# Output-weight packs of a hybrid attention + PEER layer: the last pack in group A's slot, the low parts on VectorE

## The chip, the cores and the metric

One Trainium2 chip, one NeuronCore. The metric is the device time of one execution in microseconds (us), as the median of several runs. TensorE (PE in the profile, its weight loads PEld), VectorE (DVE), ScalarE (ACT), GpSimd (POOL) and the queue of SyncE (SP), which issues all the DMAs, each work through their own instructions in order and wait for each other by semaphores.

## The reference

One decoder layer for 256 tokens of width 1024, in float32. Two groups of heads mix the tokens, their outputs go through one output projection, and a PEER feed-forward layer follows.

```python
proj = rmsnorm(x, norm1_gain) @ w_in
...
o_a = nsa_mixer(...)      # group A: compressed + selected + window attention
o_b = mla_mixer(...)      # group B: multi-head latent attention
mixed = jnp.concatenate([rmsnorm(o_a, out_gain_a), rmsnorm(o_b, out_gain_b)], axis=-1) @ w_out
h = x + mixed
return h + peer_ffn(rmsnorm(h, norm2_gain), peer_w_q, peer_sub_keys, peer_u, peer_v)
```

`w_out` is 1024 x 1024. `peer_ffn` multiplies the normalised stream by `peer_w_q`, finds the best 16 of 16,384 experts per head, and works with `peer_u` and `peer_v`, 64 MB each, in dense form.

## The kernel before, in words

**Precision by splitting.** Large products are made with `float32r` operands. Each weight tile is split into a high part, `hi` (ScalarE copies the float32 tile with rounding, line 270 or 798), and a low part, `lo` = tile - `hi` (a subtraction on VectorE or GpSimd, line 272, 796 or 801). A product is then three passes on TensorE: hi x hi, hi x lo, lo x hi. A pack of output weights is 128 x 2048 floats, 1 MB; `split_pack` gives its split a slot, and `part(q, e)` splits one quarter (128 x 512) with the low part on engine `e`, GpSimd where none is named.

**Stages.** Up to about 165 us: input projection, both attention groups, output projection, second norm. Then the PEER layer: 16 tiles of `wq` (PE rows "q"), 128 tiles of `u` ("a"), 128 tiles of `v` ("y"), each loaded, split and multiplied; TensorE goes from tile to tile. The change lies in the first part.

**Slots.** SBUF is cut into slots of 128 x 4096 floats, `slot(i, ...)`, tagged b0 to b7; a new tile in a slot waits until every reader of the old one is done. Slot 2, slot 7, slot 2 again and slot 6 hold the four packs of output weights (`wo_slot`, line 997). Slot 4 holds `aS`: group A's queries and keys (`qSa`, `kHa`, `kLa`), read only by the score matmuls "sA" (lines 676 and 677). Slot 6 holds `cm`: the compressed keys, masks, and the attention outputs by token (`otok`, ring `r_ot`), which are read up to `finish` of the last group of 128 tokens (line 604 squares them, line 608 transposes them).

**Output projection.** Packs 0 and 1 (`wo0`, `wo1`) hold the rows of group B, packs 2 and 3 (`wo2`, `wo3`) those of group A; of each pair, the first holds output columns 0 to 511 and the second 512 to 1023. `split_wo(n)` is a generator that splits a pack by quarters. `wo_mm(tt, n, ab)` makes 256 output columns for one half `tt` of the tokens and one group `ab`: 12 matmuls at line 1015 against `mixT`, the transposed outputs of the group (hi at line 613, lo at line 614), and one VectorE add into `h` (line 1019). After that follow `square` (line 1024 or 1026), the transposes of `h` ("tx", line 296), their scaling (line 298), split (299, 302), and the first `wq` tile.

**Order.** From line 993 to 1127 only SP's order is written by hand; on the other engines a scheduler sets the order from the program and its dependencies. From line 1139 on the order is the one written. SP's queue loads packs 0 to 3 (line 1001), then the first five `wq` tiles (line 783; `load(0)` to `load(4)`), each waiting for its staging buffer, which an earlier split must have read.

**Attention of group A.** `unit_A(tt, rr, g)`: scores "sA", maximum "nmA" on VectorE (line 685), exponentials on ScalarE (690), transposes "pTA" (696), evacuation "PT" (598), product with the values "oA" (708), and at the end of four heads a normalisation on VectorE (714 to 721). The eight units of the second half of the tokens go first, then the four of the first half. `end_A` adds the compressed part (line 731) and calls `finish`.

Of the kernel before, what the change touches and what calls it, by code (L numbers as in the profile page):

```python
# [85 lines left out]
def body(tc, nc, ap, dbg=None):  # L86
    V, A, T, G, S = nc.vector, nc.scalar, nc.tensor, nc.gpsimd, nc.sync
# [6 lines left out]
    with ExitStack() as ctx:  # L94
# [43 lines left out]
        def small(shape, name, dt=F32, bufs=None):  # L138
            return sm.tile(shape, dt, tag=name, name=name, bufs=bufs or 2)
# [119 lines left out]
        def split_pack(r, i, w, name):  # L259

            d = slot(i, name, F32R)
            hi, lo = d[:, :8 * w], d[:, 2048:2048 + 8 * w]
            out = (hi.rearrange("p (k n) -> p k n", k=8), lo.rearrange("p (k n) -> p k n", k=8))

            def part(q, e=None, what="hl"):

                cs = slice(q * 2 * w, (q + 1) * 2 * w)
                src = r[q // 2][:, (q % 2) * 2 * w:(q % 2 + 1) * 2 * w]
                if "h" in what:
                    A.activation(out=hi[:, cs], in_=src, func=AF.Copy)  # L270
                if "l" in what:
                    (e or G).tensor_tensor(lo[:, cs], src, hi[:, cs].bitcast(F32), op=ALU.subtract)

            def half(q, e=None, what="hl"):
                cs = slice(q * 4 * w, (q + 1) * 4 * w)
                if "h" in what:
                    A.activation(out=hi[:, cs], in_=r[q], func=AF.Copy)
                if "l" not in what:
                    return
                if (e or (V, G)[q]) is V:  # L280
                    V.tensor_tensor(lo[:, cs], r[q], hi[:, cs].bitcast(F32), op=ALU.subtract)  # L281
                else:
                    part(2 * q, G, "l")
                    part(2 * q + 1, G, "l")
            half.part = part
            return out, half
# [706 lines left out]
        with tc.manual_schedule(engines={mybir.EngineType.SP}):  # L993

            side = Side(7)
            wos = {}
            wo_slot = (2, 7, 2, 6)
            s4 = [small([128, 4], "n2_s4") for tt in range(2)]

            def load_wo(n):  # L1000
# [2 lines left out]
            def split_wo(n):  # L1003
                wos[n] = split_pack(wos[n], wo_slot[n], 256, "wo%d" % n)
                for q in range(4):
                    wos[n][1].part(q, G)
                    yield

            def wo_mm(tt, n, ab):
# [66 lines left out]
            ua = [unit_A(1, (r,), g) for r in range(4) for g in range(2)]  # L1076
            side.add(*ua[:7])
            beside(split_wo(0), 1)
            load_wo(2)
            co = compress_out()  # L1080
# [4 lines left out]
            side.add(unit_C(1), *ua[7:], ea[1], unit_C(0))  # L1085
            side.add(*[unit_A(0, rr, g) for rr in ((0, 1), (2, 3)) for g in range(2)], ea[0])
            beside(split_wo(1), 1)
            load_wo(3)
            side.until(ub[-1])
            ticks[0] = 0  # L1090
            extra += [(26, lambda: (load(0), load(1), split(0), load(2), split(1)))]
            w2g, w3g = split_wo(2), split_wo(3)
            for n in range(4):
                for tt in range(2):
# [395 lines left out]
        for s in range(NQ + NU, N):  # L1490
# [14 lines left out]
            for i, tt, n, p in order:  # L1505
                jj, (hi, lo), wh = tiles[i]
                q, src = ((0, hi), (0, lo), (1, hi))[p]
# [83 lines left out]
```

## Time and profile before

| | |
|---|---|
| median of 3 runs | 964.89 us (964.03 to 970.98) |
| profiled execution, its own time | 965.19 us |
| its span, first to last instruction | 963.4 us |
| outside the span | 1.8 us |
| granted TensorE clock, mean | 0.992 |
| first `wq` matmul (PE, line 1135) | at 164.5 us |

Times in the rows are microseconds from the span's start. A row of the timeline has start, length, engine, line, operation, output<-inputs, shape and count, and in brackets the idle time of the engine ahead of it with what ended it. A row of the table by stages has for each engine the busy time and the number of instructions that start in it, then the granted TensorE clock as a share of full speed, the share of DMA time and GB/s. A float32 matmul stands as two rows in a count.

### The profile page before, as it was taken

What the parts mean: (1) busy time and instruction counts of PE and PEld (TensorE: products, weight loads), DVE (VectorE), ACT (ScalarE), POOL (GpSimd) and SP (SyncE); (2) the same over time, 40 slices, a digit from 0 to 9 for tenths busy, and PEclk for the clock granted to TensorE, in tenths of its full rate; (3) what the DMA queues carried; (4) which work ended last, traced back from release to release, by engine and by line L of the source; (5) the groups of instructions that cost most, each with busy time, mean ns of one, the idle gap of its engine ahead of it and who ended that gap; (6) DMA issues with size and microseconds to landing.
All of it is one profiled execution on the core that took longest, in us unless ns stands there. A gap on an engine that the chain in (4) does not pass through costs nothing.

```text
span 963.4 us, 17115 instructions
## 1 busy us (share of the span) xinstructions
PE 937.8 (97%) x6651; PEld 851.0 (88%) x6651; DVE 714.3 (74%) x1346; ACT 501.2 (52%) x927; POOL 171.1 (18%) x136
## 2 busy tenths in 40 slices
PE   7999998999899999999999999999999999999998
PEld 6887787999899999999999999888888888888886
DVE  6987666777979998898999995666666666666664
ACT  4667664656354365554544544544455554445552
POOL 5333224267119400000111112000000000000000
PEclk9999998999999999999999999999999999999999
DMA  8425211654566476555555556655665655665554
GB/s 328 171 88 190 74 45 48 216 159 148 152 200 202 140 222 193 163 159 171 158 171 154 166 163 185 190 195 196 196 194 188 195 192 193 197 196 194 189 191 148
DMA packets 47314, 166.73 MB, mean 173 GB/s; under 512 B 5505, under 2 KB 6529, under 8 KB 46977
## 3 DMA queue, kind: packets, MB, share of 16 engines
q1 hardware_dynamic: 47232, 165.64, 53.9%
q8 instruction: 52, 0.85, 0.4%
q14 instruction: 30, 0.24, 0.1%
HBM read 163.52 MB, written 2.10 MB: 172 GB/s over the span
## 4 chain that ended last, share of the span: by engine, by line
PE 76%; DVE 14%; issue 4%; ACT 3%; POOL 2%; DMA 2%; SPq 0%; DVEq 0%; POOLq 0%; ACTq 0%
PE y L1508 36%; PE a L1135 26%; PE q L1135 5%; PE g L1351 3%; DVE lo L801 2%; PE wo L1015 1%; DMA raw<-u 1%; PE low L314 1%; PE s L1444 1%; DVE win L281 1%; ACT hi L798 1%; DVE B L1251 1%; PE oA L708 1%; POOL b_rs L150 1%; DVE B L1252 1%
## 5 line engine op out<-in xcount | busy, mean ns | idle before, releaser
L801 DVE TENSOR_TENSOR lo<-raw,hi 128x1024 fp32r<-128x1024 f32 x236 | 289.0, 1227 | 96.0 <-ACT hi L798 93.6
L798 ACT ACTIVATE hi<-raw 128x1024 fp32r<-128x1024 f32 x266 | 280.1, 1054 | 56.3 <-DMA raw<-u 50.1
L1508 PE MATMUL y<-hi,w 128*128 128x512 f32 x1024 | 274.6, 389 | 0.0
L1135 PE MATMUL a<-xtT,hi 128*128 128x256 f32 x2048 | 260.3, 280 | 0.0
L1135 PEld LDWEIGHTS a<-xtT,hi 128*128 128x128 f32 x2048 | 243.3, 188 | 0.4 <-issue 0.4
L1508 PEld LDWEIGHTS y<-hi,w 128*128 128x128 f32 x1024 | 192.0, 188 | 40.1 <-ACT w L1238 0.2
L1508 PE MATMUL y<-lo,w 128*128 128x512 f32 x512 | 158.4, 389 | 0.0
L1135 PE MATMUL a<-xtT,lo 128*128 128x256 f32 x1024 | 138.5, 278 | 5.0 <-DVE lo L801 5.0
L1238 ACT ACTIVATE w<-B 128x256 fp32r<-128x256 f32 x128 | 53.4, 417 | 171.2 <-PE y L1508 171.0
L1135 PEld LDWEIGHTS a<-xtT,lo 128*128 128x128 f32 x1024 | 126.8, 189 | 5.6 <-DVE lo L801 5.6
L1508 PEld LDWEIGHTS y<-lo,w 128*128 128x128 f32 x512 | 96.1, 188 | 19.9
L1239 DVE TENSOR_TENSOR w<-B,w 128x256 fp32r<-128x256 f32 x128 | 54.5, 426 | 70.0 <-ACT w L1238 70.0
L801 POOL TENSOR_TENSOR lo<-raw,hi 128x1024 fp32r<-128x1024 f32 x30 | 72.3, 2416 | 52.4 <-ACT hi L798 51.8
L1483 POOL TENSOR_TENSOR B<-gl,B 128x512 f32<-128x512 f32 (+33 forms) x37 | 29.8, 805 | 253.0 <-ACT gl L1482 253.0
L1366 ACT ACTIVATE B<-g 128x64 f32<-128x64 f32 (+29 forms) x121 | 23.7, 245 | 77.0 <-DVE B L1364 77.0
L1339 DVE TENSOR_TENSOR oh<-misc,con 128x1024 f16<-128x1024 f16 x64 | 55.9, 873 | 0.0
L1476 ACT ACTIVATE B<-a 128x512 f32<-128x512 f32 (+33 forms) x59 | 28.1, 476 | 45.1 <-PE a L1135 45.1
L1343 DVE TENSOR_TENSOR oh<-oh,gf 128x1024 f16<-128x1024 f16 x64 | 44.3, 692 | 2.2
L1351 PE MATMUL g<-oh 128*128 128x128 f16 x512 | 39.7, 220 | 0.2
L1364 DVE TENSOR_TENSOR B<-g,B 128x8 f32<-128x8 f32 (+32 forms) x69 | 32.7, 479 | 6.1 <-ACT B L1476 5.9
L1135 PE MATMUL q<-xrT,hi 128*128 128x256 f32 x256 | 35.5, 283 | 0.0
L1015 PE MATMUL wo<-wo,mix 128*128 128x256 f32 x192 | 31.8, 311 | 2.6 <-ACT mix L613 1.5
(311 smaller groups left out, 897.6 us busy)
## 6 DMA issues: line engine op xcount, KB each, us to landing
raw<-u SPq DMA_DIRECT2D x128, 512.0 KB, 3.6
raw<-v SPq DMA_DIRECT2D x128, 512.0 KB, 3.6
raw<-wq SPq DMA_DIRECT2D x16, 512.0 KB, 3.5
win<-win SPq DMA_DIRECT2D x10, 512.0 KB, 8.0
w<-w SPq DMA_DIRECT2D x8, 512.0 KB, 4.0
wo<-wout SPq DMA_DIRECT2D x8, 512.0 KB, 6.5
wsm<-wu SPq DMA_DIRECT2D x1, 1280.0 KB, 9.3
xx<-x SPq DMA_DIRECT2D x4, 256.0 KB, 3.3
```

The lines of the kernel that those rows point to most:

```text
L798: A.activation(out=hi, in_=src, func=AF.Copy)
L801: e.tensor_tensor(lo, src, hi.bitcast(F32), op=ALU.subtract)
L1015: T.matmul(o, lhsT=mixT[:, ab * 4 + c, q, tsls[tt]], rhs=ww[:, (n % 2) * 4 + c, :], start=(m == 0 and c == 0), stop=(m == 2 and c == 3))
L1135: T.matmul(out, lhsT=w[:, k, :], rhs=xT[:, k, q, :], start=(n == 0 and k == 0), stop=(n == 2 and k == 7))
L1238: A.activation(out=w[:, 0, :], in_=b, func=AF.Copy)
L1239: V.tensor_tensor(w[:, 1, :], b, w[:, 0, :].bitcast(F32), op=ALU.subtract)
L1339: V.tensor_tensor(o[:, 0:2].rearrange("p a t (i two) -> p (a t) i two", two=2), iot.rearrange("p (i two) -> p i two", two=2)[:, None].broa ...
L1343: V.tensor_tensor(pairs(o[:, 2:4]), pairs(o[:, 1:2]).broadcast_to((128, 2, 4, 64, 2)), gf[:, t4, :, :, None, :].broadcast_to((128, 2, 4, 6 ...
L1351: T.matmul(b[:, i, :], lhsT=o[:, 0, i, :], rhs=o[:, 2 + q, i, :], start=(q == 0), stop=(q == 1))
L1364: V.tensor_tensor(w, bv[:, c0:m, :], w, op=ALU.mult)
L1483: (G if j < 127 else V).tensor_tensor(dst[:, :, :td], a[:, :, :td], dst[:, :, :td], op=ALU.mult)
L1508: T.matmul(ya[tt][n], lhsT=wh[:, q, tt * 128:(tt + 1) * 128], rhs=src[:, n * 512:(n + 1) * 512], start=(jj == 0 and p == 0), stop=(jj == 1 ...
```

## The change

Two edits. The fourth pack of output weights takes slot 4 (where `aS` was) in place of slot 6 (where `cm` is). And all sixteen low-part subtractions of the four packs, 128 x 512 each, go to VectorE in place of GpSimd.

```diff
             side = Side(7)
             wos = {}
-            wo_slot = (2, 7, 2, 6)
+            wo_slot = (2, 7, 2, 4)
             s4 = [small([128, 4], "n2_s4") for tt in range(2)]
...
             def split_wo(n):
                 wos[n] = split_pack(wos[n], wo_slot[n], 256, "wo%d" % n)
                 for q in range(4):
-                    wos[n][1].part(q, G)
+                    wos[n][1].part(q, V)
                     yield
```

The scheduler also places other instructions differently. In its rows `wo_1101`, `wo_1270`, `wo_1485` and `wo_1592` are the split packs 0, 1, 2 and 3. First place: ScalarE at the end of group A's attention, where pack 3 is split. Before:

```order
L795 ACTIVATE hi<-raw 128x256
L690 ACTIVATE wsm,suA<-sA,nmA 128x128
L598 ACTIVATE PT<-pTA 128x512
L690 ACTIVATE wsm,suA<-sA,nmA 128x128 x3
L795 ACTIVATE hi<-raw 128x256 x3
L598 ACTIVATE PT<-pTA 128x512
L604 ACTIVATE fe,o_ss<-cm 128x512
L1024 ACTIVATE fe,n_s_679<-xx 128x256
L270 ACTIVATE wo_1592<-wo 128x512
L613 ACTIVATE mix<-fe 128x4x128
L270 ACTIVATE wo_1592<-wo 128x512
L299 ACTIVATE xrT<-kept 128x2x128
```

Now:

```order
L270 ACTIVATE wo_1592<-wo 128x512
L690 ACTIVATE wsm,suA<-sA,nmA 128x128
L598 ACTIVATE PT<-pTA 128x512
L690 ACTIVATE wsm,suA<-sA,nmA 128x128 x3
L270 ACTIVATE wo_1592<-wo 128x512 x2
L598 ACTIVATE PT<-pTA 128x512
L270 ACTIVATE wo_1592<-wo 128x512
L795 ACTIVATE hi<-raw 128x256 x4
L1024 ACTIVATE fe,n_s_679<-xx 128x256
L604 ACTIVATE fe,o_ss<-cm 128x512
```

The four high parts of pack 3 stood behind the square of the last attention output (line 604); they now stand among the exponentials of the last unit, ahead of it.

Second place: VectorE where group B ends and the first scores of group A arrive (from line 659 on). The difference, a piece of it:

```order
 L659 TENSOR_TENSOR cm<-oB,suB 128x512
+L272 TENSOR_TENSOR wo_1101<-wo,wo_1101 128x512 x2
+L149 TENSOR_SCALAR rs_x<-o_ss 128x1
+L611 TENSOR_TENSOR fe<-oT,pp 128x512
+L685 TENSOR_REDUCE nmA<-sA 128x2
+L272 TENSOR_TENSOR wo_1101<-wo,wo_1101 128x512
+L614 TENSOR_TENSOR mix<-fe,mix 128x4x128
+L272 TENSOR_TENSOR wo_1101<-wo,wo_1101 128x512
 L560 TENSOR_SCALAR fe<-fe 128x256
-L1019 SCALAR_TENSOR_TENSOR xx<-wo,misc,xx 128x256
+L685 TENSOR_REDUCE nmA<-sA 128x2
 L561 TENSOR_TENSOR fe<-fe,cm 128x256
```

The four low parts of pack 0 come in among group B's last `mixT` split and the first maxima of group A, and the compression's steps (lines 560, 561) fall behind them.

Third place: TensorE at the end of the projection. Before:

```order
L1015 MATMUL wo<-wo_1485,mix 128x256 x17
L608 MATMUL oT<-con,cm 128x128 x4
L296 MATMUL tx<-con,xx 128x128 x2
L1015 MATMUL wo<-wo_1485,mix 128x256 x7
L1015 MATMUL wo<-wo_1592,mix 128x256 x2
L296 MATMUL tx<-con,xx 128x128 x2
L1015 MATMUL wo<-wo_1592,mix 128x256 x15
```

Now:

```order
L1015 MATMUL wo<-wo_1485,mix 128x256 x23
L1015 MATMUL wo<-wo_1592,mix 128x256 x4
L608 MATMUL oT<-con,cm 128x128 x4
L296 MATMUL tx<-con,xx 128x128 x4
L1015 MATMUL wo<-wo_1592,mix 128x256 x20
L296 MATMUL tx<-con,xx 128x128 x2
```

Matmuls with pack 3 now stand ahead of the last `oT` transposes. SP's order is unchanged.

## The prediction

> **What bounds the kernel now.** I read the page's busy times first, then a table by stages, then, for the stage of the change, the table in finer steps and the timelines.
>
> ```profile
> PE 937.8 (97%) x6651; PEld 851.0 (88%) x6651; DVE 714.3 (74%) x1346; ACT 501.2 (52%) x927; POOL 171.1 (18%) x136
> ```
>
> ```profile
> 93.80:104.50 10.70, 9.22 (x49) 6.65 (x48) 8.22 (x12) 7.26 (x23) 8.31 (x7) 0.84 0.53 181
> 104.50:118.00 13.50, 13.50 (x103) 11.10 (x102) 7.58 (x25) 9.65 (x33) 0.74 (x1) 1.00 0.17 54
> 118.00:143.10 25.10, 24.18 (x169) 20.31 (x167) 16.73 (x44) 15.87 (x55) 5.57 (x5) 1.00 0.13 43
> 143.10:149.20 6.10, 5.98 (x44) 5.07 (x43) 5.46 (x10) 3.97 (x12) 2.43 (x3) 1.00 0.02 4
> 149.20:159.20 10.00, 5.83 (x29) 5.63 (x30) 6.27 (x11) 2.20 (x7) 5.81 (x6) 0.69 0.12 49
> 164.50:236.00 71.50, 71.50 (x621) 70.65 (x620) 53.41 (x203) 43.70 (x71) 39.31 (x24) 1.00 0.54 174
> 400.00:963.00 563.00, 559.31 (x3571) 495.97 (x3569) 399.02 (x497) 278.10 (x488) 28.75 (x33) 1.00 0.57 182
> ```
>
> TensorE is busy 97% of the span. From 164.5 on, where the PEER layer starts, it has no gap for 71.5 us, and later only small ones. So whatever brings the first `wq` matmul forward moves all that follows by as much, and the end too. Ahead of that there is one bad stage: 149.2 to 159.2, with PE busy 5.83 of 10 us and a clock of 0.69. The same stage in finer steps:
>
> ```profile
> 149.20:151.40 2.20, 1.10 (x7) 0.90 (x7) 1.37 (x3) 0.77 (x2) 2.20 (x3) 1.00 0.00 0
> 151.40:154.47 3.07, 0.00 (x0) 0.00 (x0) 3.07 (x4) 0.00 (x0) 2.34 (x2) 0.77 0.00 0
> 154.47:159.20 4.73, 4.73 (x22) 4.73 (x23) 1.83 (x6) 1.43 (x5) 1.27 (x2) 0.50 0.26 103
> 159.20:161.50 2.30, 2.30 (x19) 2.30 (x18) 0.70 (x2) 0.00 (x0) 0.00 (x0) 0.85 0.04 16
> ```
>
> PE stands still for 1.10 and 3.07 us, and then runs 4.73 us at half clock. The timelines of PE, ScalarE, GpSimd and VectorE say why:
>
> ```profile
> 150.30 1.10 PE L1015 MATMUL wo<-wo,mix 128*128 128x256 f32 x7 [1.11 <-POOL wo L272]
> 154.47 0.69 PE L296 MATMUL tx<-con,xx 128*128 128x128 f32 x2 [3.07 <-DVE xx L1019]
> ```
>
> ```profile
> 145.23 0.63 ACT L604 ACTIVATE fe<-cm 128x512 f32<-128x512 f32 x1 [3.11 <-DVE cm L731]
> 146.26 0.62 ACT L270 ACTIVATE wo<-wo 128x512 fp32r<-128x512 f32 x1
> ```
>
> ```profile
> 147.29 2.96 POOL L272 TENSOR_TENSOR wo<-wo,wo 128x512 fp32r<-128x512 f32 x2
> 150.89 2.85 POOL L272 TENSOR_TENSOR wo<-wo,wo 128x512 fp32r<-128x512 f32 x2
> ```
>
> ```profile
> 131.86 0.68 DVE L614 TENSOR_TENSOR mix<-fe,mix 128x512 fp32r<-128x512 f32 x1
> 147.43 1.69 DVE L614 TENSOR_TENSOR mix<-fe,mix 128x512 fp32r<-128x512 f32 x1
> 150.28 3.74 DVE L796 TENSOR_TENSOR lo<-raw,hi 128x256 fp32r<-128x256 f32 x3 [0.83 <-POOL wo L272]
> 153.94 0.47 DVE L1019 SCALAR_TENSOR_TENSOR xx<-wo,misc,xx 128x256 f32<-128x256 f32 x1
> ```
>
> Pack 3 is not split until 146.26, when the last reader of slot 6 (line 604, the square of the last attention output) is done. GpSimd then needs 147.29 to 153.74 for its low parts, so PE waits for them at 149.2. While GpSimd streams, VectorE's own subtractions crawl: the same line 614 takes 0.68 us with GpSimd idle and 1.69 beside it, and three small line 796 take 3.74. So the add at 153.94, for which the next transposes wait, is late, and PE stands until 154.47.
>
> **The change part by part.** *Slot.* The last reader of `aS` is this matmul:
>
> ```profile
> 136.24 0.38 PE L677 MATMUL sA<-aS 64*128 64x256 f32 x1
> ```
>
> It ends at 136.6, so the high parts can start some 9.6 us earlier than 146.26. By the new order of ScalarE they go in between the exponentials of the last unit and are over by about 142. The low parts, four on VectorE at 0.68 us (the row at 131.86 has their shape and types), are 2.7 us. VectorE has room there:
>
> ```profile
> 135.00:138.00 3.00, 3.00 (x23) 2.47 (x22) 0.69 (x1) 1.92 (x9) 0.00 (x0) 1.00 0.55 178
> 138.00:142.00 4.00, 4.00 (x35) 3.79 (x33) 1.97 (x5) 3.69 (x14) 0.00 (x0) 1.00 0.00 0
> ```
>
> 2.66 of 7 us are used. Pack 3 is then complete near 143, before PE has worked through the 24 matmuls with pack 2. So the 1.10 us stall goes, and the 3.07 one with it, as nothing of GpSimd's is left beside VectorE but small steps of line 302.
>
> *Clock.* With the two stalls gone, nothing is left that lowers the clock at 154.47. Half clock for 4.73 us costs 2.37, and 0.85 over the next 2.30 us costs 0.35: 2.7 us. The clock does not drop after every gap:
>
> ```profile
> 98.00:101.00 3.00, 3.00 (x14) 2.05 (x13) 2.96 (x5) 2.16 (x9) 3.00 (x4) 0.58 0.30 123
> 60.80:62.40 1.60, 0.00 (x0) 0.00 (x0) 1.60 (x3) 0.34 (x2) 0.00 (x0) 1.00 0.84 220
> ```
>
> From 60.8 on, a TensorE that stood still for 1.60 us kept full clock, while from 98 on it ran at 0.58. The Trainium skill, "TensorE: Matmul & The Clock Gate", section "What's actually happening", says that the clock halves after an idle window of about 3.4 us, and that these windows run freely, not tied to the kernel. The row at 154.47 agrees in kind (0.50, neither more nor less), and so does the one at 60.80. By it the cold stretch is a whole number of windows, one or two, 1.7 or 3.4 us of loss here in place of my 2.7, and a rest of the stall could still catch one; that outcome is the fourth rival below.
>
> *What stays on the path.* After the change PE runs from the last "oA" at 143.1 through pack 2 and pack 3, five groups of 12 matmuls, to the end of the first group for `tt` = 0. A group with its transposes is worth the distance of these two starts, 1.65 us:
>
> ```profile
> 161.22 1.68 PE L1015 MATMUL wo<-wo,mix 128*128 128x256 f32 x12
> 162.87 1.67 PE L1015 MATMUL wo<-wo,mix 128*128 128x256 f32 x12
> 159.29 1.95 PE L1015 MATMUL wo<-wo,mix 128*128 128x256 f32 x12
> ```
>
> Five are 8.25: done at 151.35, where the row at 159.29 (the second group for `tt` = 0) has it at 159.3. That is 7.9 us, the upper end for this part. Its operand, `mixT` for `tt` = 0, is ready by about 148.2 (line 614 at 147.43 with 0.68), ahead of the 149.7 at which it is needed. The lower end is 1.1: the pack's wait alone goes, and the adds of line 1019 stay as late. I take 1.10 + 3.07 + 2.7 = 6.9, less 0.4 for a transpose that still waits for its add (one add is 0.47): 6.5.
>
> *Sixteen low parts on VectorE.* Twelve of them (packs 0 to 2) fall between 93.8 and 143.1. Twelve at 0.68 are 8.2 us more on VectorE, where the three rows of the stage table show 32.5 of 49.3 us busy; 16.8 are free. The tight spot is the beginning: 8.22 of 10.70 us up to 104.5, with GpSimd busy 8.31 beside it. There the new order puts pack 0's four (2.7 us) among the first maxima "nmA", and PE's scores wait behind those. But this is also where GpSimd stretches VectorE's steps:
>
> ```profile
> 98.03 1.14 DVE L614 TENSOR_TENSOR mix<-fe,mix 128x512 fp32r<-128x512 f32 x1
> ```
>
> Line 614 takes 0.46 more than its 0.68, and the compression's steps move behind. So the part is costed from both sides. Latest: packs 0 and 1 whole in front of the units, 8 x 0.68 = 5.4 us later. Earliest: nothing added, and the clock kept where it now falls to 0.58 (3.0 x 0.42 = 1.3; the stretch is longer than the row, so an estimate of 1.7): 1.7 earlier. Following the new order by hand, the matmuls with group B's `mixT` start a microsecond earlier and the eight units of the second half end about where they did. I take 0.
>
> *Loads.* SP's first `wq` tiles wait for buffers that these splits read (the waits of its queue, its timeline, the page's DMA row, and ScalarE's first split of such a tile):
>
> ```profile
> SPq L783 <- POOL wo L272: 20.4, 3, 12.5
> ```
>
> ```profile
> 96.00 0.33 SPq L783 DMA_DIRECT2D raw<-wq  x1
> 127.80 0.33 SPq L783 DMA_DIRECT2D raw<-wq  x1
> ```
>
> ```profile
> raw<-wq SPq DMA_DIRECT2D x16, 512.0 KB, 3.5
> ```
>
> ```profile
> 106.21 0.72 ACT L795 ACTIVATE hi<-raw 128x256 fp32r<-128x256 f32 x2
> ```
>
> The first issues when GpSimd is through with pack 0; by the new order VectorE is through with it some 2 us later, near 98, the tile lands 3.5 us after that, and its split at 106 still finds it: no cost. The fourth, at 127.80, follows pack 2 and comes earlier.
>
> *The keys.* They are loaded into the memory of the old slots, if the big tile begins where slot 0 did into slot 4, now pack 3's:
>
> ```profile
> 166.99 0.33 SPq L1227 DMA_DIRECT2D B<-keys  x1
> ```
>
> The issue comes 2.5 us after the last matmul with pack 3 (162.87 + 1.67), and by SP's unchanged order behind the spill of that product: no cost.
>
> Sum, against the profiled execution: 965.19 - 6.5 - 0 = 958.7. That execution lies 0.3 above the median of the runs, so for a median 958.4; I say 958.5.
>
> **The rivals.** *The front gains as well.* GpSimd's contention goes and the clock does not fall at 98: 1.7 more, 956.8. If the tail reaches its 7.9 too, 965.2 - 7.9 - 1.7 = 955.6. For it: the rows at 98.03 and 98.00. Against: PE still has gaps of about a microsecond near 93 and 96 in the new order.
>
> *VectorE's queue delays the units.* Packs 0 and 1 in front of the maxima cost their 5.4 less what the contention gave, about 1.5: +3.9, so 962.5. For it: VectorE is the fullest engine up to 104.5. Against: 5.9 us of VectorE are idle from 104.5 to 118.
>
> *Slower: VectorE sets the pace to 143.* All twelve low parts land on the chain score, maximum, exponential, "oA", 8.2 us later; each makes PE wait, and the clock falls again. The tail then keeps its cold stretch: -4.2 + 8.2 = +4.0, 969.2. It decides once the last "oA" is over 6.9 us late, so with more than ten of the twelve on the path. Against: the 16.8 free microseconds.
>
> *The stall comes back elsewhere.* The slot is free but pack 3 does not come early enough, or a shorter gap remains and catches a closed clock: of 6.9 only 1.10 to 4.2 go, 961 to 964. For it: ScalarE is full from 138 to 142 (3.69 of 4), and the four high parts, 2.5 us, go there. Against: PE has 24 matmuls with pack 2 to do first, which are 3.3 us.
>
> **How the numbers follow.** The forecast, 956.5 to 961, has 0.54; the front's gain 0.16; the delayed units 0.16; the returning stall 0.09; slower 0.05. Without the outermost 0.2 the range is 954.5 to 963.8. One per cent is 9.65 us, about what a measurement of this kernel can tell from no change. Faster by over that needs below 955.2, about half of the first rival: 0.09. Slower by over 1% needs more than 974.5: only the fourth case beyond its price, 0.02. Within: 0.89.
>
> **What would show it.** In the profile after, line 270 for pack 3 starts near 137; PE has no gap over 1 us from 143 to the first `wq` matmul, with clock 1.00; that matmul stands near 158 (164.5 before); line 614 takes 0.68 each time; the last "oA" ends within 2 us of 143.1. Wrong if the last "oA" ends after 146, if PE's clock still falls to 0.50 ahead of the first `wq` matmul, or if the first `wq` matmul moves and the end does not.

## The result

The changed kernel takes 955.95 us (median of 13 runs, 953.05 to 960.89), the kernel before, measured beside it, 963.27 (13 runs, 961.28 to 973.54). The ratio is 0.9912, with a 95% interval of 0.9884 to 0.9940: 0.9% faster. The interval leaves out 1, so this is a gain, though it is smaller than the one per cent that the prediction set as its mark. Medians and ranges, here and below, are of all runs, while a ratio is not their quotient: it leaves out runs over 1.5% above the fastest of their kernel. The profiled execution took 955.38 us with a span of 953.6, 9.8 less than before.

The page's busy times, after:

```profile
PE 934.6 (98%) x6651; PEld 850.0 (89%) x6651; DVE 712.9 (75%) x1362; ACT 501.0 (53%) x927; POOL 149.5 (16%) x120
```

```profile
PE 88%; DVE 8%; ACT 1%; POOL 1%; issue 1%; DMA 0%; SPq 0%; DVEq 0%; POOLq 0%; ACTq 0%
```

VectorE has sixteen instructions more (1362 for 1346) and is busy 1.4 us *less* (714.3 before). The sixteen subtractions add 10.7 us by the sum of their rows. In return lines 560, 561, 564, 614, 721 and 796, which GpSimd had stretched, take 8.2 us less together. Another 2.3 us fall away in lines 1258 and 1263 of the PEER layer, which the change does not touch, so that part of the difference is no effect of contention with these subtractions. The second line is the head of the chain that ended last: PE has 88% of it, VectorE 8%. Before it read:

```profile
PE 76%; DVE 14%; issue 4%; ACT 3%; POOL 2%; DMA 2%; SPq 0%; DVEq 0%; POOLq 0%; ACTq 0%
```

The same stretches of time as in the prediction's table, after (the work in them has moved forward; the last one now holds the first `wq` matmul):

```profile
93.80:104.50 10.70, 10.70 (x71) 7.93 (x72) 9.49 (x19) 8.94 (x29) 0.56 (x1) 1.00 0.44 151
104.50:118.00 13.50, 13.50 (x104) 11.80 (x104) 9.36 (x32) 8.55 (x32) 0.55 (x1) 1.00 0.25 80
118.00:143.10 25.10, 24.03 (x169) 20.41 (x169) 20.26 (x52) 17.53 (x59) 0.55 (x1) 1.00 0.14 43
143.10:149.20 6.10, 5.27 (x45) 5.07 (x44) 5.63 (x15) 3.74 (x13) 1.47 (x2) 1.00 0.02 7
149.20:159.20 10.00, 10.00 (x86) 9.94 (x85) 6.34 (x23) 5.47 (x20) 4.00 (x6) 1.00 0.37 117
```

Two rows stand out. From 149.2 to 159.2 PE is busy for all of the 10 us (5.83 before) at full clock (0.69 before). From 93.8 to 104.5 it is also busy all the time (9.22 before) at full clock (0.84 before). The end of the first part, on PE's timeline:

```profile
139.61 1.00 PE L708 MATMUL oA<-xx,PT 128*128 128x64 f32 x8
...
147.98 0.44 PE L296 MATMUL tx<-con,xx 128*128 128x128 f32 x2 [0.83 <-DVE xx L1019]
...
154.77 0.48 PE L1135 MATMUL q<-xrT,hi 128*128 128x256 f32 x2
```

and before:

```profile
142.28 1.00 PE L708 MATMUL oA<-xx,PT 128*128 128x64 f32 x8
164.52 0.48 PE L1135 MATMUL q<-xrT,hi 128*128 128x256 f32 x2
```

From here on two distances are used. From the start of the last "oA" to the first `wq` matmul: 22.24 us before, 15.16 after, so the tail gained 7.08. The last "oA" itself is 2.67 earlier, so the front gained too. Together 9.75. From the first `wq` matmul to the end of the span it is 798.9 before and 798.8 after: nothing was given back later.

### The profile page after: what moved, and what is told of

It is laid out like the page before. It is cut to its first block, busy times and chain, and to the rows that moved or that the text cites. A ratio compares the mean times of both kernels' runs of the same rounds, so it can differ in the third digit from the quotient of the medians.

```text
span 953.6 us, 17117 instructions
## 1 busy us (share of the span) xinstructions
PE 934.6 (98%) x6651; PEld 850.0 (89%) x6651; DVE 712.9 (75%) x1362; ACT 501.0 (53%) x927; POOL 149.5 (16%) x120
## 4 chain that ended last, share of the span: by engine, by line
PE 88%; DVE 8%; ACT 1%; POOL 1%; issue 1%; DMA 0%; SPq 0%; DVEq 0%; POOLq 0%; ACTq 0%
PE y L1508 37%; PE a L1135 35%; PE q L1135 5%; PE g L1351 3%; PE wo L1015 2%; PE oA L708 1%; PE low L314 1%; PE ak L314 1%; PE s L1444 1%; DVE win L281 1%; DVE lo L801 1%; POOL b_rs L150 1%; PE pTA L696 1%; PE sA L677 1%; DVE rq L1417 0%
## 5 line engine op out<-in xcount | busy, mean ns | idle before, releaser
L1135 PEld LDWEIGHTS q<-xrT,hi 128*128 128x128 f32 x256 | 32.1, 188 | 0.1
```

The costliest lines, as they stand in the source:

```text
L1135: T.matmul(out, lhsT=w[:, k, :], rhs=xT[:, k, q, :], start=(n == 0 and k == 0), stop=(n == 2 and k == 7))
```

## The experiments

Each kernel was measured against the kernel before on the same chip. The first four were measured together (before: 966.06, 33 runs, 961.67 to 981.16), and so were the next four (964.24, 33 runs, 962.43 to 981.48) and the last three (964.95, 11 runs, 963.04 to 978.67).

| kernel | median, us | range | ratio and interval | last "oA" | first `wq` | distance |
|---|---|---|---|---|---|---|
| before | 963.27 | 961.28–973.54 | 1 | 142.28 | 164.52 | 22.24 |
| changed | 955.95 | 953.05–960.89 | 0.9912 [0.9884, 0.9940] | 139.61 | 154.77 | 15.16 |
| e1_slot | 961.61 | 955.31–971.77 | 0.9930 [0.9884, 0.9976] | 149.69 | 165.08 | 15.39 |
| e2_vector | 956.00 | 954.30–962.38 | 0.9905 [0.9867, 0.9942] | 141.28 | 157.88 | 16.60 |
| e3_last_on_v | 962.56 | 953.88–977.07 | 0.9929 [0.9884, 0.9974] | 158.93 | 174.15 | 15.22 |
| e4_first_on_v | 955.77 | 953.66–961.43 | 0.9892 [0.9854, 0.9930] | 141.54 | 156.44 | 14.90 |
| e5_warm | 964.49 | 962.19–968.58 | 1.0004 [0.9981, 1.0027] | 143.81 | 165.17 | 21.36 |
| e6_slot_warm | 957.69 | 954.70–960.83 | 0.9913 [0.9878, 0.9948] | 140.47 | 155.86 | 15.39 |
| e7_pack0_on_v | 963.24 | 960.46–968.70 | 0.9989 [0.9963, 1.0015] | 146.62 | 165.82 | 19.20 |
| e8_tx | 955.20 | 952.35–959.45 | 0.9897 [0.9861, 0.9933] | 142.66 | 156.95 | 14.29 |
| e9_tx_warm | 956.89 | 954.13–960.01 | 0.9900 [0.9843, 0.9956] | 142.73 | 157.03 | 14.30 |
| e10_after_again | 957.39 | 954.03–960.40 | 0.9898 [0.9841, 0.9955] | 144.94 | 160.10 | 15.16 |
| e11_tx_again | 955.20 | 954.62–961.96 | 0.9894 [0.9835, 0.9952] | 142.50 | 156.79 | 14.29 |

The last three columns come from one profiled execution each. The distance hardly depends on what happened earlier in that execution (15.16 twice for the changed kernel, with first `wq` matmuls 5.3 us apart), so it is the measure of the tail. The time of the last "oA" does depend on it.

### The two edits apart

**e1_slot**: the slot alone, all low parts on GpSimd.

```diff
-            wo_slot = (2, 7, 2, 6)
+            wo_slot = (2, 7, 2, 4)
```

> Slot 4 for the last pack alone; all low parts stay on GpSimd. Theory (two parts that add: packs 0 to 2 on VectorE bring the last oA forward by 2.7 us, and an early pack 3 takes the stalls and the half clock out of the tail, 7 us): the last oA stays where it was before (starts near 142.3), GpSimd makes pack 3's low parts from about 137 to 143 and PE does not wait for them; first wq matmul near 157.5 in place of 164.5, ratio to before 0.993. Rival 'the slot is all of it': first wq matmul near 155, ratio 0.991. Rival 'GpSimd beside VectorE is all of it': first wq matmul after 163, ratio 0.998 to 1.000.

Measured: the tail's distance falls to 15.39 with the slot alone; the two stalls and the half clock behind them are gone. In the profile all of that is lost again in front, where the last "oA" comes 7.4 us later than before. PE's timeline and the table by stages of this kernel say how:

```profile
99.36 0.74 PE L1015 MATMUL wo<-wo,mix 128*128 128x256 f32 x4 [1.49 <-ACT mix L613]
```

```profile
100.80:109.00 8.20, 8.20 (x38) 6.95 (x38) 2.92 (x4) 3.68 (x12) 2.85 (x3) 0.51 0.23 65
109.00:118.00 9.00, 9.00 (x35) 6.77 (x34) 3.51 (x13) 3.65 (x15) 0.74 (x1) 0.50 0.01 2
118.00:120.00 2.00, 2.00 (x16) 1.60 (x15) 1.05 (x4) 1.68 (x5) 0.00 (x0) 0.97 0.01 4
```

PE waited 1.49 us for group B's `mixT` (line 613), and then ran at half clock for some 17 us, busy all the time. The kernel before has the same gap, followed by only some 3.4 us at half clock in its profile (98.5 to 101.9). So after the same gap the half-clock stretch can be short or long. The record of the single runs fits that: e1's mean granted clock was 0.996 in its fastest run (955.31 us), 0.987 in the profiled one (963.66) and 0.984 in one of 966.21. What sets the length is not shown.

**e2_vector**: the low parts on VectorE alone, the slot as before.

```diff
-                    wos[n][1].part(q, G)
+                    wos[n][1].part(q, V)
```

> All sixteen low parts on VectorE; pack 3 stays in slot 6. Theory: last oA starts near 139.6 as in the changed kernel; pack 3 is split only after line 604, near 144, its four low parts take 2.7 us on VectorE, and PE waits 1 to 3 us for them; first wq matmul 157 to 159.5, ratio 0.993 to 0.995. Rival 'slot is all': first wq matmul near 164, ratio 1.000. Rival 'GpSimd beside VectorE is all of it': first wq matmul near 155, ratio 0.991.

Measured: 16.60, so this edit alone also takes away 5.6 of the tail's 7.08. What it leaves is the wait for slot 6, in PE's timeline:

```profile
146.97 1.45 PE L1015 MATMUL wo<-wo,mix 128*128 128x256 f32 x10 [0.54 <-ACT wo L270]
149.42 0.44 PE L296 MATMUL tx<-con,xx 128*128 128x128 f32 x2 [1.01 <-DVE xx L1019]
```

Pack 3's high parts are still late (they begin at 145.26, behind line 604), but VectorE follows with the low parts, three in 0.68 us and one, beside a step of GpSimd, in 1.20, and PE loses 0.54 and 1.01, without a fall of the clock. The ratio, 0.9905, is that of the full change. Group B's gap at 97 is gone here as well.

What follows: either edit alone cures the tail. They overlap, so their gains must not be added. Of the measured 0.9% the edit to VectorE alone brings all that can be resolved, and the slot alone, at 0.9930, is not apart from it by the intervals either.

### Which packs' low parts matter

**e3_last_on_v** (new slot, only pack 3 on VectorE) and **e4_first_on_v** (new slot, packs 0 to 2 on VectorE, pack 3 on GpSimd):

```diff
+                    wos[n][1].part(q, V if n == 3 else G)      # e3_last_on_v
+                    wos[n][1].part(q, G if n == 3 else V)      # e4_first_on_v
```

> Slot 4, and only pack 3's low parts on VectorE; packs 0 to 2 stay on GpSimd. Theory: last oA starts near 142.3 with the clock falling at 98 as before, tail without a stall over 1 us, first wq matmul near 157.3, ratio 0.993. If packs 0 to 2 on VectorE were no gain, it would equal the changed kernel: 155 and 0.991.

> Slot 4, packs 0 to 2 on VectorE, pack 3's low parts on GpSimd (about 134 to 141). Theory: like the changed kernel, last oA near 139.8, first wq matmul 155 to 156, ratio 0.991 to 0.992: once the slot is free early, it matters little who subtracts. Rival 'GpSimd beside VectorE': VectorE's steps at 134 to 141 are stretched by some 2 us, the last oA moves to 141.5 and the first wq matmul to 157, ratio 0.9935.

Measured: the tail is the same in both, 15.22 and 14.90. Once the slot is moved it does not matter who makes pack 3's low parts. The front is not the same. In e3, as in e1, PE has its gap of 1.48 us ahead of group B's matmuls, and half clock behind it; in e4 there is none, and its time is that of the changed kernel. (The profiled execution of e3, 977.07 us, is the longest of its runs, so of its times only the tail's distance and the gap are read.) The last "oA" of e4, at 141.54, meets the rival's number but not its reason: the clock was at half from 130.6 to 134.0, behind a gap of 1.07 us that the changed kernel has too, and this costs 1.7 of the 1.9 us by which that "oA" starts later than in the changed kernel. By the profiles, then, what the changed kernel gains in front comes from packs 0 to 2; by their ratios e3 and e4 are not apart.

**e7_pack0_on_v**: old slot, only pack 0 on VectorE.

```diff
+                    wos[n][1].part(q, V if n == 0 else G)
```

> Slot 6, only pack 0's four low parts on VectorE. Theory: they stand where GpSimd ran beside group B's last steps; with them on VectorE mixT comes a microsecond earlier, PE has no gap over 1.1 us near 97, the clock stays, last oA near 140; the tail is as before (stalls 1 and 3 us, half clock), ratio 0.997. Rival (packs 1 and 2 matter as much): last oA at 141.5 or later.

My theory, that pack 0 is all that matters in front, was wrong. The ratio is 0.9989, and the timelines of GpSimd and VectorE in this kernel show why:

```profile
96.58 3.52 POOL L272 TENSOR_TENSOR wo<-wo,wo 128x512 fp32r<-128x512 f32 x2 [11.75 <-ACT wo L270]
```

```profile
96.59 2.38 DVE L272 TENSOR_TENSOR wo<-wo,wo 128x512 fp32r<-128x512 f32 x2
100.15 0.67 DVE L272 TENSOR_TENSOR wo<-wo,wo 128x512 fp32r<-128x512 f32 x1
100.75 1.77 DVE L614 TENSOR_TENSOR mix<-fe,mix 128x512 fp32r<-128x512 f32 x1
102.44 1.76 DVE L272 TENSOR_TENSOR wo<-wo,wo 128x512 fp32r<-128x512 f32 x1
```

GpSimd, free of pack 0, starts on pack 1 at 96.58 instead, beside VectorE, and the same subtraction takes 0.67 to 0.68 us or 1.76 to 1.78 (the first row holds one of each), by how it falls beside GpSimd's subtractions, which here take 1.38 to 1.83 us themselves in place of 1.27. PE's gap for `mixT` shrinks to 0.68 us, but gaps of 0.97 and 1.88 us follow at 105 and 126, and the tail keeps a wait of 1.68 us for GpSimd's pack 3, with half clock for 3.4 us behind it. From the start of line 550's matmuls (86.88 us before, 89.77 here) to the last "oA" this execution takes 56.85 us against 55.40 before, but it also makes eight more matmuls of line 1015 in that stretch, about 1 us. Contention goes only when GpSimd is quiet, not when it does something else.

### The gap at 97 and the clock

**e5_warm** and **e6_slot_warm**: the kernel before, and e1_slot, each with one float32 matmul more that PE can do while it waits for group B's `mixT`. It fills a PSUM tile whose contents are done with, and nothing reads its result.

```diff
             V.tensor_tensor(f, b.rearrange(...), ..., op=ALU.mult)
+            if (tt, ab) == (1, 1):
+                T.matmul(b, lhsT=ident, rhs=f, start=True, stop=True)
```

> The kernel before, with one matmul more (128 x 512 float32, about 1 us, its result unused) that TensorE can do while it waits for group B's last mixT near 97. Theory 'the front's gain is the clock': the gap of 1.49 us shrinks to about 0.6, the clock stays 1.00 from 98 to 143, last oA starts near 140.5 (142.3 before), the tail's stalls and half clock stay, first wq matmul near 162.7, ratio 0.997 to 0.998 against the common runs and fewer long ones (before: up to 981 us in the last call). Rival 'the front's gain is that VectorE is no longer stretched beside GpSimd': last oA at 142 or later, ratio 1.000 or above.

> Slot 4 for the last pack and the same extra matmul near 97; every low part stays on GpSimd. Theory 'the clock': front as in the run with the extra matmul alone, tail as in the run with the slot alone (last oA to first wq matmul 15.4 us): first wq matmul near 156, ratio 0.990 to 0.992, as the changed kernel without moving one subtraction, and no run far above the others. Rival: GpSimd's contention costs by itself, first wq matmul after 158, ratio 0.994 or above.

In both, PE's gap is cut to 0.6 us, and the clock stays up. PE's timeline and stage row of e6 (the two added lines shift its later line numbers by 2):

```profile
96.88 1.13 PE L613 MATMUL oT<-fe,con 128*128 128x512 f32 x2 [0.59 <-DVE rs_x L149]
```

```profile
55.00:165.00 110.00, 104.88 (x816) 90.29 (x816) 78.50 (x200) 72.22 (x219) 35.97 (x34) 1.00 0.32 105
```

e6 is e1 with that one useless matmul. Its last "oA" comes at 140.47 in place of 149.69, its distance is the same 15.39, and its ratio is 0.9913: the changed kernel's, with all sixteen low parts still on GpSimd. (e1's ratio, 0.9930, is not apart from it by its interval, and the two were not measured together, nor on one chip. The runs behind the ratios reach 966.21 in e1 and 960.83 in e6. Whether the filler helps e1 can be read from one profile of each, not from the times.) As far as the times tell, the gain of the whole change can be had without the move to VectorE: an early pack 3, and no long gap ahead of group B's matmuls.

e5 did not show it as a time: the ratio is 1.0004. From 98 to 143 its clock is 1.00, but its profile is 2.9 us late by the start of line 550's matmuls, behind two falls of the clock, near 16 to 20 and 64 to 68, that cost some 1.7 us each:

```profile
16.40:20.00 3.60, 3.22 (x15) 3.22 (x16) 2.60 (x9) 0.00 (x0) 0.70 (x1) 0.53 0.98 405
64.00:68.00 4.00, 3.87 (x21) 3.77 (x21) 2.47 (x8) 3.34 (x17) 2.06 (x1) 0.57 0.51 170
98.00:143.00 45.00, 43.47 (x296) 34.97 (x296) 30.95 (x79) 30.86 (x105) 13.34 (x12) 1.00 0.24 73
```

Counted from the start of line 550's matmuls (86.88 before and 89.80 here) the last "oA" is 55.40 us behind it before, 54.01 here, 53.61 in e6 and 52.94 in the changed kernel. So e6 has 1.8 of the 2.5 us that the changed kernel gains in front, and e5 gained 1.4 by its profile, less than the 1.8 that I had expected; its ratio does not confirm even that. The highest of its 12 runs is 968.58, that of the 33 beside it of the kernel before 981.48; what makes this difference is not settled. With the tail's stalls left in, the filler is worth nothing that can be measured.

### What is left after the change

**e8_tx**, the changed kernel with one more edit, and the same again as **e11_tx_again** beside the changed kernel, **e10_after_again**: the last gap of the changed kernel, 0.83 us at 147.98, follows an add of VectorE that stands behind a split of the second norm (line 302) which had taken 0.95 us beside GpSimd. That split goes to GpSimd as well.

```diff
-            ... ((G, G, G, V), (G, V, G, V))[tt]) for tt in range(2)]
+            ... ((G, G, G, V), (G, G, G, V))[tt]) for tt in range(2)]
```

> The changed kernel, with one more low part of the second norm's transposes (line 302, 128 x 256) on GpSimd in place of VectorE, so that the two adds at 147.46 stand free of it. Theory: the adds come 0.9 us earlier and PE's gap of 0.83 us at 147 closes: first wq matmul 154.0 in place of 154.8, end 0.8 us earlier, ratio to the changed kernel within what can be told (0.999). Rival: GpSimd's step lies beside VectorE's and stretches it, no gain.

> The same as e8_tx (the second half's transposes scaled and split on GpSimd like the first half's), now beside the changed kernel. Theory, that the 0.87 us which the last stage lost in the profile are on the path: its median 0.5 to 1.2 us below the changed kernel's of this call. Rival: what GpSimd gives there VectorE takes later, or the difference drowns in the spread: medians within 0.4 us or the other way round.

> The changed kernel itself, beside its two variants on one chip. Theory: ratio to before 0.990 to 0.992, first wq matmul at 154 to 157 us by whether the clock falls near 62, no run above 963. Rival, that its low spread before was chance: some runs above 965, as the kernel before has them.

Measured: the gap is gone and the distance is 14.29 both times, 0.87 less than the changed kernel's 15.16, which is also the same both times. As a time it can't be told apart: the medians measured together differ by 2.2 us, which is more than the gap can give, in six runs each that spread over 6 to 7 us. The first `wq` matmul stands at 156.95 and 156.79, not at the 154.0 expected, as in both executions the clock was at half for 3.4 us twice before 70 us, which costs some 1.7 us each time. Over all runs the changed kernel has 956.05 (19 runs) and this one 955.20 (14 runs). It is the best version of this study by its profile, and by its times it is equal.

**e9_tx_warm**: e8_tx, with another matmul of this sort meant for a gap of 1.93 us near 62, where group B's first transposes wait for line 640 in every kernel.

```diff
             bt = bank("pTB")
+            if (tt, hp) == (0, 0):
+                T.matmul(bt, lhsT=ident, rhs=con[:, 0:512], start=True, stop=True)
```

> The changed kernel with the edit of e8_tx, and one more float32 matmul (128x512, its result is overwritten) ahead of group B's first transposes, where TensorE stood still for 1.93 us near 61 in every kernel so far and the clock fell behind that gap in about half of the profiles (3.4 us at half, so 1.7 us). By the new order some of the transposes of line 472 come ahead of group B's first too. My theory, that the remaining spread of the changed kernel (953 to 961) comes from clock falls behind such gaps: no gap over 1 us near 61, no clock under 0.97 between 55 and 70, first wq matmul 1 to 2 us ahead of that of e8_tx in the same call, no run above 958, ratio to before 0.986 to 0.989. Rival: VectorE and ScalarE set the pace of this stage, so the gap only moves; first wq matmul within 0.7 us of e8_tx's, a gap of 1 us or more elsewhere between 58 and 75, the same ratio within 0.002 and the same spread.

It did not close the gap. The scheduler put the matmul, whose operands are ready early, some 3 us ahead of the gap, and the gap stayed:

```profile
57.79 1.02 PE L644 MATMUL pTB<-con 128*128 128x512 f32 x2
...
63.20 0.33 PE L648 MATMUL pTB<-con,wsm 128*128 128x128 f32 x1 [1.93 <-ACT wsm L640]
```

The first `wq` matmul stood at 157.03, as in e11 (156.79). Whether closing that gap would narrow the spread of the runs (953 to 961) is open. What e10 shows of the spread: in this execution of the changed kernel the clock was at half from 18.1 to 21.5, from 65.9 to 69.3 and from 134.1 to 137.6. At 1.7 us each that is 5.1 us. The first `wq` matmul stands at 160.10, later than the 154 to 157 expected, and the whole takes 960.14 us; the first profile had none of the three (154.77, 955.38). None of its six runs is above 960.40, as expected. The clock is not all of the spread: among the 13 runs of the result, the one of 960.89 us had a mean clock of 0.995, and one of 954.92 had 0.996.

## Why the prediction was right, and where its terms were not

Predicted 958.5 (954.5 to 963.8), measured 955.95: inside the range, and 2.6 lower than the number. It lies below the forecast case proper (956.5 to 961, chance 0.54), in the first rival, to which the prediction had given 0.16. By its steps:

**Tail, 6.5 predicted: right in size, 7.08 by the distance.** By its parts, 22.24 before was 4.17 of stalls, 2.7 of lost clock and 15.37 of work. After it is 0.83 of stall and 14.33 of work. So the named causes gave 3.34 + 2.7 = 6.0 (0.83 remains where I had left 0.4). The other 1.0 was not in my sum. It is hardly work moved out of the tail: 96 matmuls of line 1015 start behind the last "oA" before and 95 after, and one is worth about 0.12. The rest is that PE worked off its matmuls at wider distances before, with pauses too short to be listed as idle. From 145.88 to 149.2 it starts 17 matmuls and 2 transposes in 3.3 us; at the distance of 0.12 us that 27 matmuls have after, these 19 would take 2.3 us. Before and after:

```profile
145.88 1.55 PE L1015 MATMUL wo<-wo,mix 128*128 128x256 f32 x9
147.53 0.44 PE L296 MATMUL tx<-con,xx 128*128 128x128 f32 x2
147.97 1.22 PE L1015 MATMUL wo<-wo,mix 128*128 128x256 f32 x8
```

```profile
140.42 3.48 PE L1015 MATMUL wo<-wo,mix 128*128 128x256 f32 x27
143.74 0.60 PE L608 MATMUL oT<-con,cm 128*128 128x128 f32 x4
```

The slot closes these pauses: with the 96 matmuls of before and full clock, PE is busy for 14.47 us of e1's tail, but for 15.06 of e2's, where pack 3 is still late.

**Slot.** Line 270 for pack 3 starts even earlier than the 137 named, on ScalarE, and the low parts follow on VectorE:

```profile
134.09 0.64 ACT L270 ACTIVATE wo<-wo 128x512 fp32r<-128x512 f32 x1
137.50 1.16 ACT L270 ACTIVATE wo<-wo 128x512 fp32r<-128x512 f32 x2
139.24 0.62 ACT L270 ACTIVATE wo<-wo 128x512 fp32r<-128x512 f32 x1
```

```profile
136.15 0.68 DVE L272 TENSOR_TENSOR wo<-wo,wo 128x512 fp32r<-128x512 f32 x1
138.18 1.29 DVE L272 TENSOR_TENSOR wo<-wo,wo 128x512 fp32r<-128x512 f32 x2
140.10 0.68 DVE L272 TENSOR_TENSOR wo<-wo,wo 128x512 fp32r<-128x512 f32 x1
```

Pack 3 is complete at 140.8. What was wrong is the division of labour that I had argued, the slot for the early split and VectorE for the contention: e1 and e2 show that each of them alone takes away both stalls, all but 0.5 and 1.0 us in e2.

**Clock in the tail, 2.7: right.** Before, it stood at half from 153.1 to 159.9, and 1.4 of these 6.8 us lay in the stall, where they cost nothing. After, it stays at 1.00 from 143 to the first `wq` matmul, and PE has no gap over 0.83 there.

**Sixteen low parts on VectorE, costed at 0: the step that was mis-sized.** The last "oA" moved by 2.67, of which 0.21 is an offset from the start of the execution. The other 2.46 lie between the start of line 550's matmuls and the last "oA", before and after:

```profile
86.88:142.28 55.40, 52.97 (x367) 42.29 (x368) 37.48 (x94) 39.57 (x124) 17.55 (x15) 0.97 0.33 111
```

```profile
86.67:139.61 52.94, 51.17 (x368) 41.28 (x369) 41.42 (x109) 40.06 (x124) 1.66 (x3) 1.00 0.35 116
```

PE is busy 1.80 us less, and 1.7 of that is what half clock cost from 98.5 to 101.9 (0.16 x 10.7 in the stage from 93.8 to 104.5). It is idle 0.66 less: before it has the gap of 1.48 and one of 0.91 at 128.9, after one of 0.69 at 93.7 and one of 1.07 at 128.4, where it waits for VectorE. With the tail's 7.08 and the offset that makes the 9.75. My bound "1.7 earlier" counted the clock and left out the gap ahead of its fall, so it was too narrow; the row was in the trace but not in my working. And the clock's part is not safe: in the profiles of e4 and of e10, the changed kernel itself, the clock fell for 3.4 us behind the gap of 1.07. VectorE's timeline before,

```profile
93.96 0.88 DVE L560 TENSOR_SCALAR fe<-fe 128x256 f32<-128x256 f32 x1 [0.17 <-ACT fe L559]
94.76 0.47 DVE L1019 SCALAR_TENSOR_TENSOR xx<-wo,misc,xx 128x256 f32<-128x256 f32 x1
95.15 1.10 DVE L561 TENSOR_TENSOR fe<-fe,cm 128x256 f32<-128x256 f32 x1
96.18 0.68 DVE L611 TENSOR_TENSOR fe<-oT,pp 128x512 f32<-128x512 f32 x1
...
99.10 1.36 DVE L564 TENSOR_SCALAR fe<-fe 128x256 f32<-128x256 f32 x1
```

ScalarE's and PE's,

```profile
97.13 0.61 ACT L613 ACTIVATE mix<-fe 128x512 fp32r<-128x512 f32 x1
```

```profile
97.80 0.73 PE L1015 MATMUL wo<-wo,mix 128*128 128x256 f32 x4 [1.48 <-ACT mix L613]
```

and VectorE's after:

```profile
93.49 1.28 DVE L272 TENSOR_TENSOR wo<-wo,wo 128x512 fp32r<-128x512 f32 x2
94.88 0.15 DVE L149 TENSOR_SCALAR rs_x<-o_ss 128x1 f32<-128x1 f32 x1
94.95 0.68 DVE L611 TENSOR_TENSOR fe<-oT,pp 128x512 f32<-128x512 f32 x1
...
96.75 0.68 DVE L614 TENSOR_TENSOR mix<-fe,mix 128x512 fp32r<-128x512 f32 x1
97.35 0.68 DVE L272 TENSOR_TENSOR wo<-wo,wo 128x512 fp32r<-128x512 f32 x1
97.95 0.28 DVE L560 TENSOR_SCALAR fe<-fe 128x256 f32<-128x256 f32 x1
```

Before, the compression's two steps (lines 560 and 561), stretched beside GpSimd, stood ahead of line 611, so `mixT` was late. After, two subtractions at full pace stand there, line 611 comes 1.2 us earlier, and group B's matmuls find their operand. Two things changed together here, the contention and the order of VectorE's steps; no run takes them apart, but e7, which has the two subtractions there with GpSimd still at work, keeps a gap of 0.68 us at this place, and the changed kernel none. The rival "the front gains as well" (956.8, or 955.6 with the tail at its upper end) is what happened. My reason against it, gaps near 93 and 96 in the new order, came to one gap of 0.69 us at 93.7, and no fall of the clock.

**Line 614 at 0.68 each time: right** (0.68, 0.68 and 0.69; 1.14 and 1.69 before). **Last "oA" within 2 us of its old place: wrong**, by the 2.67 above. **First `wq` matmul near 158: 154.8**, for the same reason.

**Loads and keys, no cost: right.** The first `wq` load issues at 98.09 (96.00 before) and the keys' load at 157.24, 2.5 us after the first `wq` matmul, and PE waits for neither. The rivals "VectorE's queue delays the units", "VectorE sets the pace" and "the stall comes back elsewhere" did not occur.

## What to carry to other kernels

Where two engines slow each other down, the price of moving work from one to the other is not its duration: count what the receiving engine gets back from the stretched steps, and look for a wait of TensorE that ends on one of those steps. Before adding the gains of two edits, ask whether each alone removes the same wait. When a term is bounded by lost clock, add the gap that starts the loss.

## What the runs showed of the hardware

**Which VectorE steps are stretched beside GpSimd.** Of the steps of 128 x 256 and more, those whose operands all lie in SBUF: line 560 takes 0.88 against 0.28 us, line 561 1.10 against 0.41, line 564 1.36 against 0.28, line 614 1.14 to 1.77 against 0.68. Those that read a PSUM operand are not: line 611 takes 0.68 and line 1019 0.47 to 0.48, beside GpSimd or not. The Trainium skill, "SBUF — State Buffer", section "SBUF: two separate sides", says that VectorE and GpSimd share one pair of ports as an exclusive lock, held for the whole instruction, and that of VectorE's steps those in a two-port mode or with two SBUF inputs need it. The rows agree in that only some kinds of steps suffer, among them those with two SBUF inputs (lines 561 and 614); that a waiting step is blocked whole is not shown, since the profile records only its longer duration.

**How long the clock stays down.** After a gap of about 1.5 us at 97 the profiles show half clock for 3.4 us (before), 17 us (e1) and 34 us (e3, in the longest of its runs), with PE busy throughout; after the gap of 1.93 us at 62, present in all kernels, it fell for 3.4 us in nine of the thirteen profiles, and not in the other four. After the gap of 1.07 us near 130 it fell for 3.4 us in two of the seven profiles that have it. So gaps of 1.1 to 1.9 us can be followed by half clock or not. The Trainium skill, "TensorE: Matmul & The Clock Gate", section "What's actually happening", has the clock return after one busy window of about 3.4 us, and the windows run freely. Free windows fit the chance in all this, and 3.4 us fits the short stretches; the 17 and 34 us, five and ten such windows, do not follow from it, and no run here settles what held the clock down.
